# Attention's output projection as seven block products ahead of the raw gate products, with the gates' sums made during the attention

## The chip, the cores and the metric

The kernel runs on one core of a Trainium2 chip. The metric is the device time of one execution in microseconds. Before the change it is 1419.86 us, the median of 3 runs (1419.58 to 1419.86). Five engines work from queues of their own: PE (TensorE: matmuls and transposes), DVE (VectorE), ACT (ScalarE), POOL (GpSimd) and SP (SyncE). SP, ACT and POOL also issue DMAs. Each engine runs its instructions in the order in which they stand; semaphores hold an instruction until others are done.

## The reference, cut to what matters

One residual block on 1024 tokens of 1024 channels, in float32:

```python
xn = rmsnorm(x, norm1_g[layer])
u = xn @ w_in[layer].astype(f32)
q_sb, k_sb, v_sb, f_raw, i_hg, q_hg, g_hg, gate_sb, gate_hg = jnp.split(u, list(c), axis=-1)
o_sb = stick_breaking_attention(split_heads(q_sb, SB_HEADS), ...)   # 8 heads of 64
o_hg = hgrn2_chunkwise(...)                                         # 4 heads of 128
o_hg = rmsnorm(o_hg, ...)
o_hg = merge_heads(o_hg) * jax.nn.silu(g_hg)
g_a = jax.nn.sigmoid(gate_sb + bg[:D_MODEL])
g_b = jax.nn.sigmoid(gate_hg + bg[D_MODEL:])
merged = g_a * (o_sb @ w_o_sb) + g_b * (o_hg @ w_o_hg)
h = x + merged @ w_out
hn = rmsnorm(h, norm2_g[layer])
h = h + jnp.square(jax.nn.relu(hn @ w_ff1)) @ w_ff2
return rmsnorm(h, final_g)
```

The change touches `o_sb @ w_o_sb` (1024 x 512 by 512 x 1024), the columns of `u` that become `g_a` and `g_b`, and where the sums of their inputs and weights are made.

## The kernel before

Every float32 product is made of three matmuls, on a high and a low part of both operands (`three`): high by high, high by low, low by high. `hi_lo` makes the two parts, a cast on ACT and a subtraction on DVE. A matmul takes 128x128 weights and 128x512 moving data; a "step" of the planner is six of them. Several large products are computed as block products with sums of blocks as operands, seven in place of eight, so the sums have to be made beforehand, by DVE or by accumulating DMAs.

The stages follow each other: norm of x and the first projections; the stick-breaking attention (8 heads, 75 to 330 us in the profile); the recurrence HGRN2 (4 heads, about 330 to 555 us); the gates with the output projection of the recurrence (`gates`); the output matrix; the MLP.

In the attention and in the recurrence PE has two lanes. "main" is the work of the stage; "fill" is work that is not urgent: projections and gate products, held in a list of jobs (`Stream`, `st`). `st.advance(n, upto)` issues n steps of the list but none past job `upto`; `st.finish(upto)` issues all up to there. In the recurrence `FILL` says how many steps go behind each piece of main work, and `upto` how far the list may run in each of five rounds. A round is `hg_levels(h)`, the scores of one head at seven levels, beside `hg_tail(h - 1)`, the output of the head before. So the order of the jobs in the list and the `upto` of each round set what stands between two pieces of main work.

Names that the prediction uses:
- `half(...)`: a 128x512 buffer out of a ring of `N_HALF = 10`; it is handed on when all that read the last content are done, a DMA to memory included. `slot(...)`: 128x1024, 40 of them.
- In `hg_levels`, level l: ACT copies the keys to a half (`ksl2_3` is head 2, level 3; line 1092), PE multiplies (`sl`), DVE and ACT lay the result into `sc`, and DVE scales k and q for the next level.
- In `hg_tail`: `pk` and `pkv` make the states, `pho{h}_{half}` the output, ACT takes squares and sums (`hon`, line 1272), POOL the root (`hn_y`, line 269), DVE the product (`hon`, line 169), PE the transposes `pot{h}_{half}`.
- `raw_job(cb)`, the raw gate products of eight column blocks: `pga` (two halves one after the other in one bank) and `pgq`; `p1` and `p14` go to memory (`pd`), `g1`, the sigmoid, to `gd`.
- `sb_job(cp)`, four jobs behind the raw gates: `pys`, two column blocks each, first half times `g1` read back from `gd`, second half plain, both to `yd`. The fourth job runs inside `gates` (`SB_HELD`).
- `sum_forms` and `whole_input`: the sums of the gates' inputs, made between the `pys` steps; the high parts are added to the low ones in place by eight accumulating DMAs (`xnl<-xnh`).
- `gates`: for each of eight pairs the products `x6`, `y5`, `x7`, `y3` (banks gX and gY), on summed inputs and summed weights.

Of the kernel before, what the change touches and what calls it, by code (L numbers as in the profile page):

```python
# [2 lines left out]

# [36 lines left out]
def kernel(  # L40
# [404 lines left out]
    class Unit:  # L445


        late = False
# [54 lines left out]
    class Stream:  # L503
        def __init__(self, eager=False):
            self.eager = eager
            self.jobs = []
            self.pos = 0
            self.gen = None
            self.steps = 0
            self.owed_t = None  # L510
# [14 lines left out]
        def prefetch(self):  # L525
            nxt = []
            for us, _ in self.jobs[self.pos + 1 :]:
                nxt += [u for u in us if u.hl is None]
                if len(nxt) >= 2:
                    break  # L530
            if nxt:
                nxt[0].split()
                if nxt[0].late and not self.jobs[self.pos][0][-1].late:
                    self.owed_t = nxt[0]
                else:
                    nxt[0].split_t()
            if len(nxt) > 1:
                nxt[1].load()

        def step(self):  # L540
# [12 lines left out]
            if next(self.gen, StopIteration) is StopIteration:  # L553
                self.gen = None
                self.pos += 1
            return True
# [657 lines left out]
    def hg_tail(h):  # L1214
# [19 lines left out]
        st.finish(j_i)  # L1234
        open_block("main")
# [72 lines left out]
    a_sb, a_hg = Split("asb"), Split("ahg")  # L1308
# [38 lines left out]

    def gate_bias(which, cb):
        return prm[:, BG + which * KT + cb : BG + which * KT + cb + 1]

    def gate_cols(which, cb):
        if cb < KT:
            c0 = (C_GA, C_GB)[which] + cb * P
        else:
            c0 = C_GH + (2 * (cb - KT) + which) * P
        return slice(c0, c0 + P)

    class RawUnit(Unit):
# [5 lines left out]
        def __init__(self, cb):  # L1364
            dmas = [
                [(0, P, W_IN[:, gate_cols(w, cb)].rearrange("(k p) c -> p k c", p=P))]
                for w in range(2)
            ]
            super().__init__(f"wga{cb}", dmas)
            if cb < KT:  # L1370
                self.roomy = (1,)

        def split(self):
            if self.hl is not None:
                return
            self.load()
            ra, rb = self.raw
            h, l = (
                wpool.tile([P, 1024], F32R, tag=t, name=f"{self.name}{t}") for t in ("whi", "wlo")
            )  # L1380
            hi_lo(h, l, ra)
            self.hl = [(h, l)]

        def split_t(self, behind=None, upto=3):
            ra, rb = self.raw
            while self.turned < upto:
                self.turned += 1
                if self.turned == 1:
                    after(sub(rb, ra, rb), behind)
                elif self.turned == 2:  # L1390
                    after(sub(rb[:, 512:], rb[:, 512:], rb[:, 0:512]), behind)
                else:
                    t = slot(f"{self.name}t", F32R)
                    self.hl.append((t[:, 0:512], t[:, 512:]))
                    after(hi_lo(*self.hl[1], rb[:, 512:]), behind)
# [3 lines left out]
    def raw_job(cb):  # L1399
        u = raw_units[cb]  # L1400

        def steps_of(ps, wt, w0, half_, k0, start):
            wh, wl = u.hl[wt]
# [8 lines left out]

        def body():
            p1, p14, g1 = (half(f"{n}_{cb}") for n in ("p1", "p14", "g1"))
            ps, p4 = bank(f"pga{cb}"), bank(f"pgq{cb}")
            if 6 <= cb < KT:
                load_g1(cb - 6)
            if 5 <= cb < KT:
                sb_units[cb - 5].load()
            if 3 <= cb < KT - 1:  # L1420
                osb[cb - 3] = slot(f"osr{cb}")
                load(osb[cb - 3], od[cb - 3])
            yield from steps_of(ps, 0, 0, 0, 0, True)
# [5 lines left out]
            yield from steps_of(p4, 1, 0, 1, 4, True)  # L1429
            add(p14, p1, p4)  # L1430
            if cb == 3 or cb == KT - 1:
                whole_input(1, int(cb == KT - 1))
            nc.gpsimd.dma_start(pd[cb][:, 1, :], p14)
            yield from steps_of(ps, 0, 4, 0, 4, False)
            if cb < KT:
                nc.scalar.activation(g1, ps, AF.Sigmoid, bias=gate_bias(0, cb))
            else:
                nc.scalar.activation(g1, ps, AF.Sigmoid)
                mul(g1, ps, g1)
            nc.scalar.dma_start(gd[cb], g1)  # L1440
            if 4 <= cb < KT:
                a_sb.put(cb - 4, osb.pop(cb - 4))
# [3 lines left out]
    side, g1r = [], {}  # L1446
# [5 lines left out]
    forms, whole = {}, {}  # L1452
    WAIT = 7

    def whole_input(i, j):
        for kp in range(2):
            h, l = (t.bitcast(F32) for t in xn.t[i, 2 * j + kp])
            nc.gpsimd.dma_start(l, h, accum_op=ALU.add)
            whole[i, j, kp] = l

    def sum_forms():


        raw = whole
        def split(m, kp, src):
            forms[m, kp] = tuple(slot(f"gs{n}{m}{kp}", F32R) for n in "hl")
            hi_lo(*forms[m, kp], src)

        for j in range(2):
            whole_input(0, j)  # L1470
        yield from range(WAIT)
        s1, s2 = {}, {}
        for kp in range(2):
            s1[kp] = slot(f"gs1{kp}")
            ins = add(s1[kp], raw[1, 0, kp], raw[1, 1, kp])
            if kp == 0:
                after(ins, hg_sum[0])
            yield
        for kp in range(2):
            split(5, kp, s1[kp])  # L1480
            yield
        for kp in range(2):
            s2[kp] = slot(f"gs2{kp}")
            sub(s2[kp], s1[kp], raw[0, 0, kp])
            yield
            split(6, kp, s2[kp])
            yield
        gates_in[0].load()
        gates_in[0].load_sums()
        for kp in range(2):  # L1490
            s3 = slot(f"gs3{kp}")
            sub(s3, raw[0, 0, kp], raw[1, 0, kp])
            split(7, kp, s3)
            yield
        gates_in[0].split()
        for kp in range(2):
            s4 = slot(f"gs4{kp}")
            sub(s4, raw[0, 1, kp], s2[kp])
            split(3, kp, s4)
            yield  # L1500
        gates_in[1].load()

    sb_units = []

    def sb_job(cp):
        src = W_OSB[:, cp * 256 : (cp + 1) * 256].rearrange("(k p) c -> p k c", p=P)
        unit = Unit(f"wo0{cp}", [[(0, 256, src)]])
        unit.roomy = (0,)
        sb_units.append(unit)

        def body():
            if cp == 0:
                side.append(sum_forms())
            for j in range(2):
                cb = 2 * cp + j
                if 1 < cb + 1 < KT:
                    load_g1(cb + 1)
                g1 = g1r[cb]
                for i, cs in halves():
                    ps = bank(f"pys{cb}_{i}")  # L1520
                    for _ in proj_half(
                        ps, unit.hl[0], a_sb.mov, 4, i, lambda k: k * 256 + j * P
                    ):
                        next(side[0], None)
                        yield
                    if i == 0:
                        mul(g1, ps, g1)
                        nc.gpsimd.dma_start(yd[cb][:, i, :], g1)
                    else:
                        y = half(f"ys{cb}")  # L1530
                        nc.scalar.copy(y, ps)
                        nc.scalar.dma_start(yd[cb][:, i, :], y)

        return st.add([unit], body)
# [17 lines left out]
    j_raw = [raw_job(cb) for cb in range(KT)]  # L1552
    j_sb = [sb_job(cp) for cp in range(4)]

    class GatePair:
# [3 lines left out]
        def load(self):  # L1559
            cb = self.cb  # L1560
            self.raw = [
                wpool.tile([P, 1024], F32, tag="raw", name=f"wg{cb}r{i}") for i in range(2)
# [26 lines left out]
        def split(self, behind=None):  # L1589
# [4 lines left out]
            after(sub(r0[:, s0], r0[:, s1], r0[:, s0]), first)  # L1594
            sub(r1[:, s0], r1[:, s1], r0[:, s0])
# [8 lines left out]
            sub(r0[:, s1], r1[:, s1], r0[:, s1])  # L1604
# [33 lines left out]
        def gated(self, which, first, second):  # L1638
# [11 lines left out]
            if which == 0:  # L1650
                muls()
# [16 lines left out]
        def x7(self):  # L1668
            self.product(7, self.X, False)
            p1, p14 = self.p[:, 0:512], self.p[:, 512:1024]  # L1670
            self.y_sum = add(p1, p1, self.Y)
            add(p1, p1, self.X)
# [15 lines left out]
        def y3(self):  # L1688
            self.product(3, self.Y, False)
            add(self.u2, self.u2, self.Y)  # L1690
# [52 lines left out]
    SB_HELD = {KT: 4}  # L1743
# [7 lines left out]
    def gates():  # L1751
        for v, n, m in zip(gates_in, gates_in[1:] + [None], gates_in[2:] + [None] * 2):
# [8 lines left out]
            st.advance(SB_HELD.get(v.cb, 0), j_sb[3])  # L1761
# [4 lines left out]
            st.finish(j_sb[3])  # L1766
# [632 lines left out]
    wsums = out_weight_sums()  # L2399
    done = 0  # L2400
    for i, it in enumerate(items):
# [52 lines left out]
    st.finish(j_sb[2])  # L2454
    for _ in side[0]:
# [100 lines left out]
```

## Time and profile before

| | |
|---|---|
| median of the runs | 1419.86 us |
| the profiled execution | 1420.01 us |
| its span, first to last instruction | 1418.2 us |
| granted TensorE clock, mean | 0.999 |
| DVE busy, attention (75 to 330 us) | 186.8 of 255 us |
| DVE busy, 420 to 510 us | 71.6 of 90 us |
| data moved by DMA | 241.91 MB |

All durations below come from that one execution; its own time is 1.8 us over its span. In rows of the timeline and of the groups stand start and duration in microseconds, the engine, the line of the program, the operation, what it writes and reads, the shape, and in brackets how long the engine sat idle before and what ended that. In the chain in order of time a row is start, duration, engine, bank and the number of instructions. In the rows by stretch stand the stretch, its length, then busy time and number of instructions of PE, of PE's weight loads, DVE, ACT and POOL, the granted clock, the DMA engines' busy share and GB/s (where the view is asked for PE alone, the other engines are missing). A row of DMA issues ends with the median time from issue to landing.

### The profile page before, as it was taken

Reading aid. Unit: us, or ns where it says so; the run is one execution under the profiler, and the core shown is the slowest. Engines: PE = TensorE matmul, PEld = TensorE weight load, DVE = VectorE, ACT = ScalarE, POOL = GpSimd, SP = SyncE. Lnnn points to the kernel's source line nnn. Section 1 sums busy time; section 2 is a strip of 40 time slices with the busy share of each in tenths; the row PEclk is TensorE's granted clock in tenths of the full one; section 3 lists DMA queues with packets and bytes.
Section 4 is the critical chain, followed back from the end, with each engine's and each line's share of the span. In section 5 each row is a group of like instructions: output and inputs, shape, how many; then the busy total and the mean of one; then the engine's idle time right before and its main releaser. Section 6 shows DMA issues by size and latency. Waiting matters only on the chain.

```text
span 1418.2 us, 18602 instructions
## 1 busy us (share of the span) xinstructions
PE 1408.0 (99%) x6848; PEld 1183.5 (83%) x6848; DVE 1049.5 (74%) x1429; ACT 659.3 (46%) x1127; POOL 145.0 (10%) x282
## 2 busy tenths in 40 slices
PE   9999999999999999999999999999999999999998
PEld 7888888888888888888888888888888888888886
DVE  6667777778567888887788897676766657668765
ACT  6455555554243554433244764445444443534343
POOL 3011223110011031000000300000000000000042
PEclk9999999999999999999999999999999999999999
DMA  8344445435135685364585514444446974776725
GB/s 253 83 119 127 104 101 102 104 77 154 60 75 169 224 223 186 120 214 156 162 298 194 186 53 170 163 163 142 138 145 239 351 269 148 278 274 242 273 97 186
DMA packets 169730, 241.91 MB, mean 171 GB/s; under 512 B 30844, under 2 KB 97960, under 8 KB 169640
## 3 DMA queue, kind: packets, MB, share of 16 engines
q1 hardware_dynamic: 151432, 192.48, 41.0%
q0 software_dynamic: 11616, 34.61, 9.9%
q10 hardware_dynamic: 6592, 13.63, 2.7%
q8 instruction: 54, 0.88, 0.3%
q14 instruction: 36, 0.29, 0.1%
HBM read 170.43 MB, written 68.16 MB: 168 GB/s over the span
## 4 chain that ended last, share of the span: by engine, by line
PE 97%; ACT 1%; DMA 1%; DVE 1%; issue 0%; POOL 0%; SPq 0%; POOLq 0%; DVEq 0%; ACTq 0%
PE pm L128 21%; PE pX L128 9%; PE pW L128 6%; PE pY L128 6%; PE pjqk L128 6%; PE pga L128 4%; PE gX L128 4%; PE gY L128 4%; PE pjf L128 3%; PE pjq L128 3%; PE pys L128 3%; PE pji L128 3%; PE pyh L128 3%; PE po L128 3%; PE z L128 2%; PE pwX L128 2%
## 5 line engine op out<-in xcount | busy, mean ns | idle before, releaser
L854 DVE TENSOR_TENSOR_SCAN rm<-rm,bits 128x512 f32<-128x512 f32 (+6 forms) x72 | 87.5, 1222 | 30.5 <-ACT rm L835 29.0
L156 ACT CAST whid<-w 128x1024 fp32r<-128x1024 f32 x30 | 31.6, 1054 | 153.8 <-PE pm L128 85.4
L128 PE MATMUL pm<-wlod,sh 128*128 128x512 f32 x240 | 93.6, 390 | 0.0
L128 PE MATMUL pm<-whid,sl 128*128 128x512 f32 x240 | 93.5, 389 | 0.0
L128 PE MATMUL pm<-whid,sh 128*128 128x512 f32 x240 | 93.4, 389 | 0.0
L128 PE MATMUL pm<-tl,sh 128*128 128x512 f32 (+1 forms) x210 | 81.3, 387 | 0.0
L128 PE MATMUL pm<-th,sl 128*128 128x512 f32 (+1 forms) x210 | 81.3, 387 | 0.0
L128 PE MATMUL pm<-th,sh 128*128 128x512 f32 (+1 forms) x210 | 81.3, 387 | 0.0
L161 DVE TENSOR_TENSOR wlod<-w,whid 128x1024 fp32r<-128x1024 f32 x30 | 36.7, 1222 | 55.0 <-ACT whid L156 54.8
L156 ACT CAST wTh<-pw 128x512 fp32r<-128x512 f32 (+2 forms) x96 | 43.7, 482 | 62.4 <-PE pw L131 60.8
L161 DVE TENSOR_TENSOR wTl<-pw,wTh 128x512 fp32r<-128x512 f32 (+2 forms) x96 | 50.5, 548 | 28.9 <-ACT wTh L156 28.6
L161 DVE TENSOR_TENSOR sl<-sa,sh 128x1024 fp32r<-128x1024 f32 x56 | 68.2, 1218 | 0.6 <-ACT sh L156 0.6
L2173 POOL TENSOR_SCALAR fss<-fss 128x1 f32<-128x1 f32 x8 | 4.3, 543 | 562.0 <-ACT fsc L2168 561.5
L156 ACT CAST sh<-sa 128x1024 fp32r<-128x1024 f32 x56 | 57.2, 1045 | 7.8 <-DMA sa<-ad 7.8
L128 PEld LDWEIGHTS pm<-wlod,sh 128*128 128x128 f32 x240 | 45.1, 188 | 9.9 <-DVE wlod L161 0.4
L128 PEld LDWEIGHTS pm<-whid,sh 128*128 128x128 f32 x240 | 45.0, 188 | 9.4
L128 PEld LDWEIGHTS pm<-whid,sl 128*128 128x128 f32 x240 | 45.1, 188 | 9.2
L128 PE MATMUL pX<-sqh,t1l 128*128 128x512 f32 x128 | 50.0, 390 | 0.0
L128 PE MATMUL pX<-sql,t1h 128*128 128x512 f32 x128 | 50.0, 390 | 0.0
L128 PE MATMUL pX<-sqh,t1h 128*128 128x512 f32 x128 | 49.8, 389 | 0.0
L128 PEld LDWEIGHTS pm<-th,sh 128*128 128x128 f32 x210 | 39.5, 188 | 8.1
L128 PEld LDWEIGHTS pm<-tl,sh 128*128 128x128 f32 x210 | 39.4, 188 | 8.0
(936 smaller groups left out, 4358.8 us busy)
## 6 DMA issues: line engine op xcount, KB each, us to landing
w<-in_w_ff_dram SPq DMA_DIRECT2D x72, 512.0 KB, 4.8
sa<-ad SPq DMA_DIRECT2D x52, 512.0 KB, 6.8
ad<-a SPq DMA_DIRECT2D x32, 256.0 KB, 4.5
ad<-s SPq DMA_DIRECT2D x16, 512.0 KB, 3.2
tw<-in_w_out_dram POOLq DMA_DIRECT2D x24, 256.0 KB, 5.8
pr<-pd SPq DMA_DIRECT2D x10, 512.0 KB, 5.8
x<-in_x_dram SPq DMA_DIRECT2D x8, 512.0 KB, 7.9
xnl<-xnh POOLq DMA_DIRECT2D x8, 512.0 KB, 6.2
```

Of the source, the lines that this page charges most:

```text
L128: return pe(nc.tensor.matmul(*a, **k))
L156: hi_last[0] = after(in_turn("act", nc.scalar.copy(dst, src)), hi_behind[0])
L161: nc.vector.tensor_tensor(out=dst, in0=src, in1=hi.bitcast(F32), op=ALU.subtract),
L854: sc = nc.vector.tensor_tensor_scan(out=rr, data0=rr, data1=bits[:, 1024 - nk + a : 1024 - nk + b][:, ::-1], initial=rm[:, b : b + 1] if i ...
L2173: nc.gpsimd.tensor_scalar(out=ssq, in0=ssq, scalar1=1.0 / D, scalar2=EPS, op0=ALU.mult, op1=ALU.add)
```

## The change

The output projection is now seven block products over a 2x2 split (`SB_ORDER` 2, 5, 1, 6, 7, 4, 3), with four column blocks (`cp`) each of six matmuls: 168 matmuls in place of 192. It stands ahead of all eight raw gate products in the list of jobs (`j_sb` ahead of `j_raw`). The products are combined in halves a2, a5, a6 and stored to `yd` before the gate is known; `last` in the raw gate product reads them back (`y0`) and multiplies. Its weight sums (`tv`) and the fourth weight sums of the gates (`tg4`) are made by DMAs on POOL's queue during the attention, and the sums of the gates' inputs (`xs`, stored to `sx`) by 20 DVE operations of 128x1024 during the attention. The raw gates run in the order `RAW_ORDER`; the second-half products of the last four (`HELD`) run inside `gates`, in place of the last quarter of the projection. The signs of several sums in the gates are turned with that. The core of the diff:

```diff
+    def input_sums():
+        def step(out, a, b, op):
+            after(nc.vector.tensor_tensor(out=out, in0=a, in1=b, op=op), turn_lo[0])
+        def stored(m, kp, t):
+            nc.gpsimd.dma_start(sx[m][kp], t)
         for kp in range(2):
...
+            s = slot(f"xs{kp}")
+            step(s, h00, h10, ALU.subtract)
+            yield
...
+            stored(7, kp, s)
...
+    SB_ORDER = (2, 5, 1, 6, 7, 4, 3)
...
+        def end(m, cp, ps):
+            if m in (2, 5, 4):
+                t = half(f"a{m}{cp}")
+                nc.scalar.copy(t, ps)
+                if m == 4:
+                    nc.scalar.dma_start(yd[cp][:, 1, :], t)
+                    return
+                sb_sum[m, cp] = t
+            elif m == 1:
+                t = sb_sum.pop((2, cp))
+                add(t, t, ps)
+                nc.gpsimd.dma_start(yd[cp][:, 0, :], t)
+            elif m == 6:
+                t = sb_sum[6, cp] = half(f"a6{cp}")
+                sub(t, sb_sum[5, cp], ps)
+            elif m == 7:
+                t = sb_sum.pop((5, cp))
+                sub(t, t, ps)
+                nc.gpsimd.dma_start(yd[cp + 4][:, 1, :], t)
+            else:
+                t = sb_sum.pop((6, cp))
+                add(t, t, ps)
+                nc.gpsimd.dma_start(yd[cp + 4][:, 0, :], t)
...
+            for m in ms:
+                n = SB_ORDER.index(m)
+                ahead = SB_ORDER[n + 1 : n + 3]
+                for cp in range(4):
+                    end(m, cp, product(m, cp))
...
+        def last(ps, hl, w0):
+            yield from steps_of(ps, hl, w0, 0, 4, False)
+            g1 = half(f"g1_{cb}")
+            if cb < KT:
+                nc.scalar.activation(g1, ps, AF.Sigmoid, bias=gate_bias(0, cb))
+                mul(g1, g1, y0.pop(cb))
+                nc.gpsimd.dma_start(yd[cb][:, 0, :], g1)
...
-    j_raw = [raw_job(cb) for cb in range(KT)]
-    j_sb = [sb_job(cp) for cp in range(4)]
+    j_sb = [sb_job(ms) for ms in ((2, 5), (1, 6, 7, 4, 3))]
+    j_raw = [raw_job(cb) for cb in RAW_ORDER]
+    j_held = held_job()
...
-    SB_HELD = {KT: 4}
+    SB_HELD = {KT: 4, KT + 1: 5}
...
-        if i % 2 == 1:
+        if i % 16 != 0:
             next(wsums, None)
+        if i > 2 and i % 5 > 1:
+            next(insums, None)
...
-        upto = (j_i, j_raw[1], j_raw[6], j_sb[1], j_sb[2])[h]
+        upto = (j_i, j_sb[0], j_raw[1], j_raw[6], j_raw[7])[h]
...
-    st.finish(j_sb[2])
-    for _ in side[0]:
+    st.finish(j_raw[7])
+    for _ in st.side:
         pass
     gates()
```

How the rows of instructions moved. PE, in the recurrence at head 2, level 2 (`sl_2`; pga is the raw gate product). Before:

```order
L128 MATMUL pga_4433<-xnh_261,wga1whi 128x512
L128 MATMUL pga_4433<-xnl_262,wga1whi 128x512
L128 MATMUL sl_2_4494<-q_3623,ksl_2_4492 128x128 x4
L128 MATMUL pga_4433<-xnh_261,wga1wlo 128x512
L128 MATMUL pga_4433<-xnh_261,wga1whi 128x512
```

PE at the same level now (pys_4577 is product 1, column block 1, and pys_4604 its block 2; the six matmuls of block 0 stand directly ahead of the six of block 1):

```order
L129 MATMUL pys_4577<-asl_4313,wo1whi 128x512
L129 MATMUL pys_4577<-ash_4312,wo1wlo 128x512
L129 MATMUL sl_2_4594<-q_3689,ksl_2_4592 128x128 x4
L129 MATMUL pys_4604<-ash_4312,wo1whi 128x512
L129 MATMUL pys_4604<-asl_4313,wo1whi 128x512
```

Raw gate matmuls around the level have become matmuls of product 1.

ACT at the same place, with what each row waits for (an engine's name, DMAHW for a DMA issued by SP or ACT, DMASW for one issued by POOL; `a` are the halves of the projection). Before:

```order
L156 CAST wga2whi<-wga2r_4366 128x1024 [waits DMAHW2_49]
L1425 DMA pd_112<-p_1_4430 128x512 [waits Activation_49]
L156 CAST wga2t<-wga2r_4368 128x512 [waits DMAHW4_49,DVE_49]
L1092 COPY ksl_2_4492<-k_3370 128x2x64x4
L1436 ACTIVATE g_1_4432<-pga_4433,prm 128x512 [waits PE_49]
L1440 DMA gd_122<-g_1_4432 128x512 [waits Activation_49]
```

And now:

```order
L157 CAST wo6whi<-wo6r 128x1024 [waits DMAHW5_49,PE_49]
L1688 COPY a_4542<-pys_4535 128x512 [waits PE_49]
L157 CAST ash_4719<-osr_4188 128x512 [waits DVE_49]
L1279 ACTIVATE hon_0_4546,hss_0_4545<-pho_0_4544 128x128 [waits PE_49,Activation_49,Pool_49]
L1279 ACTIVATE hon_0_4546,hss_0_4545<-pho_0_4544 128x128 x3
L157 CAST ash_4719<-osr_4196 128x512
L1097 COPY ksl_2_4592<-k_3438 128x2x64x4 [waits DMASW3_49,DVE_49]
L157 CAST wo7whi<-wo7r 128x1024 [waits DMAHW6_49,PE_49]
```

The copy for level 2 had no wait of its own and now has one for a DMA of POOL's queue; by the semaphore's count that DMA is the store of a20 (product 2 plus product 1, column block 0) to `yd`. The copy for level 3 waits in the same way for the store of a50 (product 7, column block 0).

PE at the end of the recurrence, head 3. Before, 18 pys stand between pho_1 and pot_0, and 12 between pot_0 and pot_1, which ends:

```order
L128 MATMUL pys_1_5519<-asbh_5121,wo02h_5237 128x512
L128 MATMUL pys_1_5519<-asbl_5122,wo02h_5237 128x512
L128 MATMUL pys_1_5519<-asbh_5121,wo02l_5238 128x512
L131 MATMUL pot_1_5535<-ident,hon_1_5465 128x128 x4
L128 MATMUL gX_5541<-gsh_5323,whig_5433 128x512
```

Now:

```order
L129 MATMUL pho_1_5580<-v_3861,sc_4906 128x128
L129 MATMUL pho_1_5580<-k_4217,q_4338 128x128
L132 MATMUL pot_0_5614<-ident,hon_0_5544 128x128 x4
L132 MATMUL pot_1_5620<-ident,hon_1_5582 128x128 x4
L129 MATMUL gX_5642<-gsh_5346,whig_5499 128x512
L129 MATMUL gX_5642<-gsl_5347,whig_5499 128x512
```

No fill is left between pho_1, the two groups of transposes and the first gate product.

More of the change, by code (lines that the diff above doesn't have):

```diff
@@ L2 @@
 from contextlib import ExitStack
+from itertools import chain
 import concourse.bass as bass
@@ L555, in step @@
                 self.pos += 1
+            next(self.side, None)
             return True
@@ L1503 @@
[L1503 to L1509, printed above, removed]
-        def body():
[L1512 to L1534, printed above, removed]
+    forms = {}
@@ new lines, in sb_load, with sb_split @@
+    def sb_load(m):
+        plain = {1: (0, 0), 2: (1, 0), 3: (1, 1)}
+        sums = {5: 1, 7: 3, 6: 2, 4: 4}
+        src = sb_block(*plain[m]) if m in plain else tv[sums[m]]
+        sb_raw[m] = wpool.tile([P, 1024], F32, tag="raw", name=f"wo{m}r")
+        load(
+            sb_raw[m].rearrange("p (k c) -> p k c", k=2),
+            src.rearrange("(k p) c -> p k c", p=P),
+        )
+    def sb_split(m):
+        sb_w[m] = tuple(
+            wpool.tile([P, 1024], F32R, tag=t, name=f"wo{m}{t}") for t in ("whi", "wlo")
+        )
+        hi_lo(*sb_w[m], sb_raw.pop(m))
@@ L2453 @@
             st.finish(max(j_f[h + 1], j_q[h + 1]))
-    st.finish(j_sb[2])
-    for _ in side[0]:
+    st.finish(j_raw[7])
+    for _ in st.side:
         pass
```

308 lines of the change are left out of this document (229 added, 79 removed).

## The prediction

> **What bounds the kernel now.** I read the page first, then who waits for what on PE, then busy time by stretch, then the chain in order of time, then the DMA landings.
>
> ```profile
> span 1418.2 us, 18602 instructions
> ...
> PE 1408.0 (99%) x6848; PEld 1183.5 (83%) x6848; DVE 1049.5 (74%) x1429; ACT 659.3 (46%) x1127; POOL 145.0 (10%) x282
> ...
> PE 97%; ACT 1%; DMA 1%; DVE 1%; issue 0%; POOL 0%; SPq 0%; POOLq 0%; DVEq 0%; ACTq 0%
> ```
>
> The profiled execution took 1420.01 us, 1.8 us more than its span; the median of the three runs shown is 1419.86. PE is busy 99% of the span and is 97% of the chain that ended last. Its waits are all at the start:
>
> ```profile
> PE warm L128 <- POOL ident masks.py:199: 2.3, 1, 2.3
> PE xnt L131 <- DVE x L653: 0.4, 1, 0.4
> ```
>
> The stretches that the change touches are full, by busy time for each of the engines:
>
> ```profile
> 75.00:330.00 255.00, 254.94 (x1456) 220.72 (x1455) 186.82 (x244) 143.55 (x327) 55.48 (x134) 1.00 0.49 109
> 420.00:510.00 90.00, 90.00 (x487) 77.14 (x486) 71.59 (x117) 41.02 (x92) 13.72 (x20) 1.00 0.65 193
> 510.00:600.00 90.00, 90.00 (x442) 75.44 (x441) 75.63 (x107) 42.27 (x73) 10.74 (x15) 1.00 0.61 182
> ```
>
> The first bracketed pair is PE: 90.00 of 90. So the kernel gets shorter only by PE work removed, and any new wait on PE is paid in full, since nowhere later does PE have idle time to give it back. The question is thus: how many matmuls go, and where does PE wait in the new order.
>
> **Matmuls removed.** Before, the attention's output projection is 8 column blocks x 2 halves x 12 = 192 matmuls of 128x512. Seven products x 4 column blocks x 6 = 168 replace them. The rest of PE's program has the same instructions, moved. The price, from the chain in order of time (the row with 24 matmuls), with the end of the recurrence stage, which is needed below:
>
> ```profile
> 545.40 1.78 PE pho L128 x16
> 547.18 4.10 PE pys L128 x18
> 551.28 0.44 PE pot L131 x4
> 551.72 2.77 PE pys L128 x12
> 554.49 0.44 PE pot L131 x4
> ...
> 560.40 5.44 PE pys L128 x24
> ```
>
> 24 matmuls cost 5.44 us (0.2267 each): **-5.44 us**. A group of six is 1.36 us.
>
> **Work added in the attention.** Twenty sums of 128x1024 on DVE for the gates' inputs, 8 stores of 512 KB and 24 DMAs of weight sums on POOL's queue. DVE has 255.00 - 186.82 = 68.2 us free there, and such a sum costs
>
> ```profile
> 447.42 1.22 DVE L1317 TENSOR_TENSOR wga3r<-wga3r,wga3r 128x1024 f32<-128x1024 f32 x1
> ```
>
> 1.22 us, so 24 us in all: the free time hides it. One sum can come ahead of a product that PE is about to need, but only when PE's cover there is below 1.22 us. I take +0.4, between 0 and 2.5 (two sums in full at bad places). The POOL issues stand on an engine that is 22% busy there, and nothing of the stage reads what they write.
>
> **Waits added behind stores.** This is the main term. The new products end in halves (128x512 buffers), and ten halves serve everything: a2, a5, a6, the copies of k for the recurrence's levels (ksl), hon. A half that is stored to yd through POOL's queue is free when the store has landed. In the new order ACT's copy of k for level 2 of head 2 carries a wait on POOL's DMA queue: its half is a20's, which DVE finishes only after product 1, block 0, and PE wants that level after one more group of six. The copy for level 3 gets the half of a50, two groups of six behind product 7, block 0. Before, the same kind of wait is harmless:
>
> ```profile
> 432.24 0.58 POOL L1433 DMA_DIRECT2D pd<-p  x1 [11.56 <-DVE k L1249]
> ...
> 448.94 0.65 ACT L1092 COPY ksl<-k 128x512 f32<-128x512 f32 x1
> ```
>
> The store stands 16.7 us ahead of the copy that takes its half. Now the hand-offs, row by row:
>
> ```profile
> 444.06 0.68 DVE L1314 TENSOR_TENSOR p<-p,pgq 128x512 f32<-128x512 f32 x1
> 445.04 0.63 POOL L1433 DMA_DIRECT2D pd<-p  x1 [2.76 <-DVE p L1314]
> ...
> 458.01 0.61 ACT L1092 COPY ksl<-k 128x512 f32<-128x512 f32 x1
> 458.67 1.16 PE L128 MATMUL sl<-q,ksl 128*128 128x128 f32 x8
> ```
>
> DVE's sum takes 0.68, POOL issues 0.30 after its end (445.04 - 444.74), ACT's copy takes 0.61, PE starts 0.05 behind it (458.67 - 458.62): 1.64 us beside the landing. The landings of 256 KB through POOL's queue, asked for 425 to 445, 445 to 460, 460 to 480 and 480 to 500 us:
>
> ```profile
> pd<-p POOLq DMA_DIRECT2D x1, 256.0 KB, 4.1
> ...
> pd<-p POOLq DMA_DIRECT2D x2, 256.0 KB, 5.7
> ...
> pd<-p POOLq DMA_DIRECT2D x2, 256.0 KB, 4.0
> ...
> pd<-p POOLq DMA_DIRECT2D x1, 256.0 KB, 2.3
> ```
>
> Weighted, (4.1 + 11.4 + 8.0 + 2.3) / 6 = 4.3 us.
> Level 2: 1.64 + 4.3 - 1.36 = 4.6. Ahead of a20's sum DVE also has a 128x1024 and a 128x512 operation queued, 1.22 + 0.68 = 1.9 us if it is behind, 0 if not; DVE is 80% busy there before (71.59 of 90) and gets more work, so I add 1.2: **+5.8 us** (2.6 with a landing of 2.3 and no queue, 7.9 with 5.7 and the whole queue). Behind this copy on ACT stand the cast of the next weights and hon's squares; both have more than a group of six to go, so they shift with PE.
> Level 3: 1.64 + 4.3 - 2.72 = **+3.2 us** (1.2 to 5.3, with one 0.68 ahead).
> Three more places wait for such stores with a cover about as long as the chain (a63 ahead of product 7's last block, the copy for level 5, hon of head 1): **+0.8 us** together (0 to 1.5).
>
> **A wait at the end of the recurrence.** hon is the normed output of a half of a head: squares on ACT, root on POOL, product on DVE. Before, 30 pys matmuls and four transposes stand between the last pho and the second pot (547.18 to 554.49). In the new order pot_0, pot_1 and the gates follow pho_1 directly, so PE waits for hon less the four transposes. The shortest and the longest such latency:
>
> ```profile
> 438.08 1.56 PE pho L128 x14
> ...
> 442.32 0.69 DVE L169 TENSOR_TENSOR hon<-pho,hn_y 128x512 f32<-128x512 f32 x1 [3.63 <-ACT wga2whi L156]
> ...
> 552.71 0.69 DVE L169 TENSOR_TENSOR hon<-pho,hn_y 128x512 f32<-128x512 f32 x1 [0.93 <-POOL hn_y L269]
> ```
>
> 442.32 + 0.69 - 439.64 = 3.37, and 553.40 - 547.18 = 6.22. Less 0.44: 2.9 to 5.8. The long one had two casts of 128x1024 among its squares, and in the new order ACT has none there, so I take the short side: **+3.2 us**.
>
> **What moves without a price.** Half of the second-half products of the raw gates (48 matmuls) moves into the gates, where a quarter of the output projection (48 pys matmuls) stood: PE does as much there as before, and the gates' own order around it is the same. Their products with y0 need a load of 256 KB from yd that SP issues one block of 12 matmuls (2.72 us) or more ahead; nothing on PE waits for their result but a bank. If that load were late by its whole landing it would hold DVE, which is not full in that stretch (75.63 of 90), and PE only behind it, so I cost it at 0. The removed accumulating DMAs, subtractions and g1 traffic all stood beside a full PE: 0.
>
> **The sum.** -5.44 + 0.4 + 5.8 + 3.2 + 0.8 + 3.2 = +8.0 on 1420.01: **1428.0 us**, 0.6% slower. All low ends: -5.44 + 0 + 2.6 + 1.2 + 0 + 2.9 = +1.3, 1421.3. All high ends: -5.44 + 2.5 + 7.9 + 5.3 + 1.5 + 5.8 = +17.6, 1437.6.
>
> **The rivals.**
> Short landings: with every store near the 2.3 of one row, levels 2 and 3 cost 3.8 and 1.2 and the near ties nothing: -5.44 + 0.4 + 3.8 + 1.2 + 3.2 = +3.2, 1423.2. For it: the DMA engines carry less then, since raw gate loads come later. Against: five of six rows. [...]
>
> The clock falls while PE waits. These are PE's busy time, matmuls and granted clock at both ends of the span:
>
> ```profile
> 3.00:4.00 1.00, 1.00 (x7) 1.00 1.04 401
> ...
> 5.00:6.00 1.00, 1.00 (x9) 1.00 1.11 282
> ...
> 1412.00:1418.20 6.20, 0.00 (x0) 0.76 0.59 209
> ```
>
> After the last matmul the granted clock means 0.76 over 6.20 us; if the lower step is a half, it fell for 0.24 x 6.20 / 0.5 = 3.0 us, so some 3.2 us into the idle time. A level-2 wait of 5.8 us is longer. At the start PE does 7 matmuls in a microsecond and later 9, so a restart costs some 0.7 us, and up to 1.6 at half speed for 3.2 us: 1428.0 + 1.5 = 1429.5. Against it: the clock is recorded as 1.00 in that start, so the price is not shown. [...]
>
> The ring has a free half: if levels 2 and 3 get halves whose stores landed long ago, as the row of 16.7 us shows for the kernel before, both waits are gone and the near ties too: -5.44 + 0.4 + 3.2 = -1.8, 1418.2, not slower. It decides at a cover of 1.64 + 4.3 = 5.9 us between store and use; the new order has 1.36 and 2.72, which speaks against it.
>
> No new wait binds at all: -5.4, 1414.6. That would need the pot wait hidden too, against a shortest latency of 3.37.
>
> **Chances.** Forecast 0.45, clock 0.22, short landings 0.17, free half 0.08, no wait 0.08. A measurement of this kernel tells about 0.2% from no change, 2.8 us: same is 1417.0 to 1422.7. Faster is the last rival and a little of the free half: 0.09. Same is most of the free half and half of the short landings: 0.16. Slower is the rest, 0.75. The range goes from the free half, 1418, to 1434, six above the forecast: the clock and half of the high ends together. It leaves out the no-wait case and some 0.1 above.
>
> **What would show it.** In the new profile, PE's waits should have rows for sl behind ksl, 8 to 10 us in two long pieces, and for pot behind hon, about 3 us, and ACT's ksl should wait for DMA of yd. The attention should end where it does now. If PE's waits stay at the start only, the forecast is wrong as a whole; if they are there but short, the landing was mis-sized; if the clock is below 1.00 after a wait, the clock rival is right.

## The result, and the profile after

The changed kernel takes 1439.41 us, the median of 4 runs (1438.11 to 1440.66), beside 1419.86 (1419.58 to 1420.27) for the kernel before: a ratio of 1.0137, interval 1.012 to 1.0155. It is 1.4% slower. The prediction was 1428.0 in a range of 1418 to 1434: slower was right, the size was not, and the time lies outside the range. The profiled execution took 1438.38 us, so 18.4 more than that of before, with a span 18.0 longer.

The page of the changed kernel, with the span, the busy times and the chain's shares by engine:

```profile
span 1436.2 us, 18699 instructions
...
PE 1409.7 (98%) x6824; PEld 1182.0 (82%) x6824; DVE 1066.1 (74%) x1463; ACT 667.9 (47%) x1147; POOL 165.4 (12%) x318
...
PE 93%; ACT 2%; DMA 2%; issue 1%; DVE 1%; POOL 1%; SPq 0%; POOLq 0%; ACTq 0%; DVEq 0%
```

24 PE instructions are gone, as the change says. But PE is 93% of the chain where it was 97%, and ACT and DMA, with 2% each, have twice their share. Its waits (total, how often, the longest):

```profile
PE sl L129 <- ACT ksl L1097: 11.3, 5, 4.8
PE pot L132 <- DVE hon L170: 3.0, 1, 3.0
...
PE po L129 <- DVE wTl L162: 0.8, 1, 0.8
```

The three stretches that were full before (busy times of PE, PE's loads, DVE, ACT, POOL; then clock, DMA share, GB/s):

```profile
75.00:330.00 255.00, 253.91 (x1449) 219.35 (x1448) 203.39 (x260) 143.24 (x325) 78.47 (x166) 1.00 0.76 173
420.00:510.00 90.00, 81.06 (x409) 67.95 (x408) 66.78 (x113) 39.05 (x77) 10.71 (x19) 0.96 0.42 138
510.00:600.00 90.00, 84.60 (x431) 70.53 (x430) 64.70 (x102) 44.86 (x94) 10.59 (x18) 0.98 0.59 196
```

PE now idles 1.1, 8.9 and 5.4 us in them, 15.4 in all, which agrees with the waits in the view above (15.1). The granted clock is below 1.00 in the last two. The five waits of `sl`, one row each in the timeline (start, duration; the bracket is PE's idle time before):

```profile
436.73 1.18 PE L129 MATMUL sl<-q,ksl 128*128 128x128 f32 x8 [0.94 <-ACT ksl L1097]
...
448.25 1.16 PE L129 MATMUL sl<-q,ksl 128*128 128x128 f32 x8 [3.25 <-ACT ksl L1097]
...
468.25 2.08 PE L129 MATMUL sl<-q,ksl 128*128 128x128 f32 x8 [4.75 <-ACT ksl L1097]
...
532.66 1.16 PE L129 MATMUL sl<-q,ksl 128*128 128x128 f32 x8 [1.28 <-ACT ksl L1097]
...
540.83 1.16 PE L129 MATMUL sl<-q,ksl 128*128 128x128 f32 x8 [1.09 <-ACT ksl L1097]
```

The first three are levels 1, 2 and 3 of head 2, the last two levels of head 3. What held them, by the chain in order of time (start, duration, what):

```profile
444.90 2.60 DMA yd<-a
...
447.58 0.63 ACT ksl L1097
...
462.48 5.03 DMA yd<-a
...
467.58 0.63 ACT ksl L1097
...
470.33 0.85 PE pot L132 x4
471.18 3.99 PE pys L129 x11
...
565.74 1.15 ACT hon L1279 x8
...
568.32 0.70 DVE hon L170
...
569.07 0.66 PE pot L132 x4
569.72 4.33 PE gX L129 x12
```

Both long waits of head 2, levels 2 and 3, go through a store to `yd` that has to land before ACT may overwrite its half, and the wait of `pot` goes through the squares, the root and the product of `hon`. These are the three places that the prediction named. (`pot` and `pys` at 470 us come right behind the eight `sl` of 468.25.) But those eight take 2.08 us behind the wait at level 3 and 1.16 behind the one at level 2. The rows of PE alone show why (length, PE busy and matmuls, clock, DMA share, GB/s; the lower six are cut where PE starts or stops and where the clock changes):

```profile
444.90:447.50 2.60, 0.10 (x1) 1.00 0.76 292
462.48:467.51 5.03, 1.02 (x5) 0.99 0.90 294
...
463.50:467.39 3.89, 0.00 (x0) 1.00 1.00 332
467.39:474.22 6.83, 5.97 (x20) 0.50 0.05 19
474.22:477.00 2.78, 2.78 (x14) 1.00 0.27 100
...
569.07:569.79 0.72, 0.72 (x5) 1.00 1.04 399
569.79:573.21 3.42, 3.42 (x10) 0.50 1.10 362
573.21:576.00 2.79, 2.79 (x14) 1.00 0.15 57
```

The clock fell to a half at 467.39, while PE waited, and came back only at 474.22. Behind the wait of `pot` it fell too, from 569.79 to 573.21, although PE had started again at 569.07. What that costs follows from the chain: 2.08 + 0.85 + 3.99 = 6.92 us at level 3, against 0.89 (eight `sl` at full clock, seen in an experiment below) + 0.44 + 11 x 0.2267 = 3.82, so 3.1; and 0.66 + 4.33 against 0.44 + 12 x 0.2267 at `pot`, 1.8.

The other three waits of `sl` have no store ahead of them. They stand behind ACT's own queue, here in the timeline for the two of head 3 (at level 1 it is a copy out of `pys` and two casts):

```profile
531.41 0.69 ACT L1460 ACTIVATE g<-pga,prm 128x512 f32<-128x512 f32 x1 [0.71 <-PE pga L129]
532.00 0.61 ACT L1097 COPY ksl<-k 128x512 f32<-128x512 f32 x1
...
539.22 1.04 ACT L157 CAST gsh<-gs 128x1024 fp32r<-128x1024 f32 x1
540.15 0.62 ACT L1097 COPY ksl<-k 128x512 f32<-128x512 f32 x1
```

No copy has idle time of ACT before it (no bracket): ACT was busy with a gate's sigmoid, which itself had waited for the gate's product (0.71), and a cast of the gates' inputs.

In the rows by stretch above, the first two are the two landings. The longer one, 5.03 us, moved over a DMA system that was 90% busy, the shorter one, 2.60 us, over 76%.

The end of the program. After the last matmul the changed kernel has 7.90 us (1428.30 to 1436.20) and the kernel before 6.40 (1411.80 to 1418.20), with the same work: DVE, ACT and POOL are busy 2.0, 2.4 and 1.3 us in it, before 2.0, 2.5 and 1.3. What differs is a DRAIN on POOL's queue, an instruction that stands behind all of POOL's work. Before, in the changed kernel, and in the run below in which SP issues the stores of products 1 and 7 (a row has the number of such instructions, the shortest, median and longest in ns, the first and last start in us):

```profile
L2551 POOLq DRAIN  x3: 46/102/2516, 1413.1 to 1417.9; - x3
...
L2758 POOLq DRAIN  x3: 46/102/5823, 1429.6 to 1436.0; - x3
...
L2758 POOLq DRAIN  x3: 50/93/5166, 1431.5 to 1437.2; - x3
```

The long one lasts 2.5 us where POOL issues 133 DMAs in the program, 5.8 where it issues 169, and 5.2 with 161. In the changed kernel it ends at 1435.4, behind SP's wait for the last output, which is over at 1434.4. Before it ended at 1415.7, and SP's wait came last, at 1417.4. So the longer end goes with the 36 DMAs that POOL issues more; why the DRAIN grows with them the runs don't show.

**Where the 18.0 us of span come from:**

| | predicted | measured |
|---|---|---|
| 24 matmuls removed | -5.4 | -5.4 |
| attention (idle 1.09 less 0.06) | +0.4 | +1.0 |
| head 2, level 1 (in the prediction: near ties) | +0.8 | +0.9 |
| head 2, level 2 | +5.8 | +3.3 |
| head 2, level 3 | +3.2 | +4.8 |
| head 3, two levels | 0 | +2.4 |
| `pot` behind `hon` | +3.2 | +3.0 |
| clock at a half behind two waits | 0 | +4.9 |
| behind the last matmul | 0 | +1.5 |
| sum | +8.0 | +16.4 |

The rest, 1.6 us, is mostly PE's restart behind a wait at full clock: at level 2 eight `sl` take 1.16 us and not 0.89, so 0.27 each time, for some five waits.

### The profile page after: what moved, and what is told of

The parts are those of the page before. It is cut to its first block, busy times and chain, and to the rows that moved or that the text cites. A ratio compares the mean times of both kernels' runs of the same rounds, so it can differ in the third digit from the quotient of the medians.

```text
span 1436.2 us, 18699 instructions
## 1 busy us (share of the span) xinstructions
PE 1409.7 (98%) x6824; PEld 1182.0 (82%) x6824; DVE 1066.1 (74%) x1463; ACT 667.9 (47%) x1147; POOL 165.4 (12%) x318
## 4 chain that ended last, share of the span: by engine, by line
PE 93%; ACT 2%; DMA 2%; issue 1%; DVE 1%; POOL 1%; SPq 0%; POOLq 0%; ACTq 0%; DVEq 0%
PE pm L129 21%; PE pX L129 9%; PE pW L129 6%; PE pY L129 6%; PE pjqk L129 5%; PE gX L129 4%; PE pga L129 4%; PE gY L129 4%; PE pjf L129 3%; PE pji L129 3%; PE pyh L129 3%; PE pjq L129 3%; PE po L129 3%; PE pwX L129 2%; PE pjv L129 2%; PE z L129 2%
## 5 line engine op out<-in xcount | busy, mean ns | idle before, releaser
L840 ACT ACTIVATE rm<-z 128x512 f32<-128x512 f32 (+3 forms) x96 | 44.3, 498 | 7.0 <-DMA sx<-xs 4.2
```

Of the source, the lines that this page charges most:

```text
L840: scored[0] = nc.scalar.activation(rm[:, s0 : s0 + m], z[:, :m], AF.Sigmoid, scale=-0.125)
```

## The experiments

The theory is the prediction's, corrected in size: the halves that wait for stores (8 us at two levels), the clock behind the second of them, the lost cover of `hon`, the DVE sums of the attention. The main rival is that a wait only moves when its cause is taken away. A question beside it is what makes a landing long, the queue or the place. Each ratio is against the kernel before on the same chip. In these kernels some line numbers are one higher than in the changed one.

### Keys in halves of their own

```diff
-    N_FULL, N_HALF = 40, 10
+    N_FULL, N_HALF = 39, 10
...
+    kpool = ctx.enter_context(tc.tile_pool(name="keys", bufs=2))
...
-            keys = slot_n(f"k{name}", 512)
+            keys = kpool.tile([P, 512], F32, tag="k", name=f"k{name}")
```

> The copies of k for the recurrence's levels get two halves of their own; one full buffer less pays for them (39 instead of 40); all else as in the change. Theory (the copies of levels 2 and 3 of head 2 wait for a half whose store has to land): the two long waits of PE for sl, 3.4 and 4.9 us, are gone, and with the second one the half clock behind it (2.9 us): 11.2 us less than the change, about 1428. Rival (the copies are late because ACT, DVE or POOL are late there, and the store only ends last): another wait takes their place, less than 4 us gained.

1427.36 us (1426.3 to 1428.31), ratio 1.0053 (1.0036 to 1.007): 12 us less than the changed kernel, from one decision on buffers. No wait of `sl` is left, and the clock holds where it had been halved; a row of PE alone:

```profile
468.00:470.00 2.00, 2.00 (x15) 1.00 0.99 389
```

So the halves do cause the waits of head 2. Those of head 3 go too, but there the trace shows another order on ACT: the copies for the two levels (523.24 and 527.54 in this run) now stand ahead of the sigmoid (524.04) and of the cast (530.69), and not behind them. What remains in PE's waits is the lost cover of `hon`, and two new ones in the attention:

```profile
PE pot L133 <- DVE hon L171: 3.0, 1, 3.0
...
PE pjq L130 <- DVE wTl L163: 2.2, 1, 2.2
PE z L130 <- ACT osb L935: 1.3, 1, 1.3
```

The chain shows how these two come about (the last row, from the recurrence, is that of eight `sl` at full clock):

```profile
150.12 8.88 DMA sx<-xs
...
159.14 5.36 DMA od<-osb
...
165.37 1.91 PE pjq L130 x6
...
457.85 0.89 PE sl L130 x8
```

Behind the wait of `pjq` the clock fell once more: six `pjq` take 1.91 us in place of 1.36 and the next twelve 3.40 in place of 2.72, and the mean granted clock over the attention is 0.99 here and 1.00 in the changed kernel. The keys' space came out of the ring of 40, and with 39 the attention waits for a store of an input sum. That was tried by itself, next.

### One 128x1024 buffer fewer, nothing else

The edit is `N_FULL` 39 alone.

> The change with 39 full buffers instead of 40 and nothing else. Theory (the first experiment's attention ended later because the 40th full buffer is needed there, by the sums of the input): about 4 us slower than the change, some 1443, all of it before 330 us. Rival (that delay came from the moved order of issue and not from the buffer): the same as the change, 1439.

1442.73 us (1439.35 to 1443.4), ratio 1.0155 (1.014 to 1.0171), 3.3 above the changed kernel. In the stretch of the attention PE is busy 250.74 of 255 us, against 253.91 in the changed kernel: 3.2 us. So the loss in the attention above belongs to the buffer. Between the two kernels with 39 buffers, with and without halves for the keys, lie 15.4 us.

### Keys in one half, taken from the ring of halves

The same pool with `bufs=1`, and `N_HALF` 9, so that no other ring shrinks.

> The change with one half of its own for the copies of k and nine in the ring: the memory of the change exactly, 40 full buffers. Theory (the shared ring is the cause, and the attention of the first experiment lost some 4 us to the missing full buffer): the waits for levels 1 to 3 of head 2 and the half clock are gone and the attention is that of the change: 1439 - 1.1 - 3.4 - 4.9 - 2.9 = about 1427, or 1424 if the two waits of head 3 go too, as they did in the first experiment. Rival (nine halves are too few for a2, a5, a6 and hon): DVE or ACT wait for stores there and PE behind them, over 1431.

1432.54 us (1431.29 to 1433.96), ratio 1.0089 (1.0074 to 1.0104): the rival, in part. The keys don't wait any more. Instead ACT waits for halves of `hon` (6.7 us in two waits) and DVE for a half of product 6 (2.7), each held by a store, and PE waits behind DVE at product 7:

```profile
PE pys L130 <- DVE a L1325: 5.8, 3, 2.9
```

5.8 us of waits in place of 8.0, and no more: whoever takes a half out of this ring next has to wait for a landing. It is the number of halves against the time that a store holds one, not the keys as such.

### No sums of the gates' inputs

```diff
-            s = slot(f"xs{kp}")
-            step(s, h00, h10, ALU.subtract)
...
+            for m, src in ((7, h00), (6, h10), (3, h01), (5, h11)):
+                for _ in range(2):
+                    yield
+                stored(m, kp, src)
+                yield
```

> The change without the 20 sums of 128x1024 on DVE in the attention; eight stores of 512 KB remain, but of plain parts of the input, so that the gates get unsummed inputs. Theory (one such sum stands ahead of a wTl and of a q that PE waits for at 167 and 161 us): the attention ends 1.1 us earlier, as before the change, about 1438.3. Rival (the DMAs of the sums, which nearly double the traffic there, are what is late): no gain.

1438.09 us (1436.92 to 1438.56), ratio 1.0128 (1.0113 to 1.0143), 1.3 below the changed kernel, whose runs and these overlap. PE is busy 254.94 of 255 us in the attention, as before the change. That says more than the two medians, for in this run's profile the clock also fell behind level 2 (eight `sl` in 2.08 us), which it did not in the changed kernel's. In the changed kernel the place is (timeline)

```profile
164.84 1.21 DVE L1522 TENSOR_TENSOR xs<-xs,xnl 128x1024 f32<-128x1024 f32 x1
165.98 1.21 DVE L162 TENSOR_TENSOR wqk5l<-wqk5r,wqk5h 128x1024 fp32r<-128x1024 f32 x1
167.11 0.87 DVE L162 TENSOR_TENSOR wTl<-pw,wTh 128x512 fp32r<-128x512 f32 x2
167.84 0.38 PE L129 MATMUL po<-wTl,V 128*128 128x256 f32 x1 [0.79 <-DVE wTl L162]
```

One of the twenty sums stands ahead of a subtraction that PE waits for, on an engine that is 80% busy (203.39 of 255). The other nineteen cost nothing that shows.

### Cover for the normed output at the end of the recurrence

`FILL` of the last round from 2.9 to 1.9, which leaves fill matmuls between the last `pho` and `pot`.

> The change with 1.9 in place of 2.9 steps of fill per piece in the last round of the recurrence, so that 12 of the 48 raw gate matmuls left there stand between the last pho and the first pot, and 6 between the two pots (4.1 us). Theory (hon's latency has no cover): PE's wait for hon of 3.15 us is gone, and the half clock behind it (1.7 us): 4.9 us less, about 1434.5. Rival (the products taken away ahead of pkv and pho uncover waits there): less than 3 us gained, with new waits for pp or k.

1435.89 us (1434.88 to 1437.21), ratio 1.0114 (1.0099 to 1.0129): 3.5 below the changed kernel, where 4.9 were expected. The wait of `pot` and the fall of the clock behind it are gone (the clock is 1.00 over 510 to 600 us). Of the other 1.4, 1.0 stands in its waits as two new ones, `pkv` behind ACT (0.7) and the gates' `gX` behind DVE (0.3): the fill that was moved had covered them.

### Matmuls in place of the idle time

Twenty matmuls of 128x512 into the bank of level 3, meant to keep PE busy through the wait there.

```diff
+            for _ in range(20 if name == "sl2_3" else 0):
+                matmul(S, ones, xn.mov(0, 0)[0], start=True, stop=True)
```

> The change, with 20 matmuls of 128x512 on operands that are ready, put on PE directly ahead of head 2's level 3, into the bank that the level then overwrites: 20 x 0.2267 = 4.5 us of PE work that falls into the 4.9 us wait. Theory (the matmuls of 0.43 us behind that wait come from the granted clock, which falls because PE is idle): the clock stays at 1.00 there and the 2.9 us are gone, about 1436.5. Rival (they are slow because of what DVE, ACT and the DMAs do then): the same slow matmuls, no gain, or a loss where the wait is shorter than 4.5 us.

1442.82 us (1442.35 to 1445.04), ratio 1.0166 (1.0151 to 1.0181). This says nothing on the question, for the order of PE's program did not put them where they were meant to be. In its timeline (the second row; the first is level 2) they stand ten microseconds ahead of the wait:

```profile
447.58 2.08 PE L129 MATMUL sl<-q,ksl 128*128 128x128 f32 x8 [3.09 <-ACT ksl L1097]
...
458.65 4.70 PE L129 MATMUL sl<-xnh,ones 128*128 128x512 f32 x20
```

The wait at level 3 (4.43 us) and the half clock (0.50 from 472 to 476 us) stayed, and the 20 matmuls came on top. The run shows something else by chance: the wait at level 2, here 3.09 us, is followed by eight `sl` in 2.08 us, so the clock fell, which it did not behind 3.25 us in the changed kernel's profile. The last section has the rows of both.

### Stores by SP in place of POOL

```diff
-                nc.gpsimd.dma_start(yd[cp][:, 0, :], t)
+                nc.sync.dma_start(yd[cp][:, 0, :], t)
...
-                nc.gpsimd.dma_start(yd[cp + 4][:, 1, :], t)
+                nc.sync.dma_start(yd[cp + 4][:, 1, :], t)
```

> The change, with the eight stores of products 1 and 7 to yd issued by SP in place of POOL; the ring and the order of the products as in the change. Theory (the two long waits are the store's landing and little else: landings of 2.6 and 5.0 us gave waits of 3.4 and 4.9): with SP's stores near the 2.0 to 2.7 of its other stores of 128 to 256 KB the second wait falls to some 2.5 us and no longer drops the clock: 2.4 + 2.9 less, about 1434; the first stays near 3. Rival (the landing depends on what the DMA engines carry then, not on the queue; or SP, held by the wait for DVE, brings the next weights late): no gain, or new waits for loads.

1439.48 us (1437.61 to 1439.62), ratio 1.0135 (1.012 to 1.015): no gain in the time. The chain's two landings:

```profile
445.70 2.92 DMA yd<-a
...
464.71 4.71 DMA yd<-a
```

2.92 and 4.71 where POOL's queue had 2.60 and 5.03: at these two places the landing hardly depends on the queue. The equal time is a sum of small things. In this run's profile the wait at level 3 is 0.6 shorter and the end 0.7, but the attention idles 1.0 more, and the clock fell behind level 2 as well (a wait of 3.05, then eight `sl` in 2.07).

### The causes taken together

First the keys in one half and `FILL` 2.4 in each of the last three rounds.

> One half of its own for the copies of k, nine in the ring, and 2.4 steps of fill per piece in the last three rounds of the recurrence (2.6, 2.6, 2.9 in the change), so that 24 raw gate matmuls stand between the last pho and the last pot. Theory (ring and fill are all that the change lacks): no wait of PE over 1 us from 330 to 600 us and the clock at 1.00: 1427 less 4.9 for hon and its clock, less 2.9 for head 3, about 1419, where the 24 matmuls saved are half spent by the attention's 1.1 and near ties. Rival (with the ring tight, waits only move): over 1424.

1426.75 us (1424.5 to 1428.51), ratio 1.0047 (1.003 to 1.0064), and not 1419. What is left is one wait of 3.0 for the half of product 6's last block, which a store holds (4.90 us in the chain), with twelve `pys` behind it that take 4.60 us where twelve at full clock take 2.72, and small waits. Then also the stores by SP, and the sums of the inputs behind other pieces of the attention (`i % 5 < 3` in place of `i % 5 > 1`).

> The kernel of both ring and fill, with products 1 and 7 stored by SP, and with the sums of the input stepped at the items 0, 1, 2 of each five in place of 2, 3, 4. Theory: the wait of 3.2 us for a63 (its half too waits for a store) falls under 2 us, and the sums no longer stand ahead of the wTl and q of 161 and 167 us (1.9 us): 1426.8 less 1.5 less up to 1.9, about 1424. Rival (the sums hold some other item of the attention instead, and the shorter store only uncovers DVE): 1426 to 1428.

1421.27 us (1419.8 to 1424.04, 10 runs), ratio 1.0011 (1.0001 to 1.002), the clock at 0.999 as before the change. In the attention PE is busy 254.80 of 255 us, with all twenty sums in it. What each of the two edits gives on this kernel was not tried apart. Last, two other fills on top of that, 2.4, 2.5, 2.5 and 2.4, 2.6, 2.1.

> Keys in a half of their own with nine halves in the ring, products 1 and 7 stored by SP, the sums of the gates' inputs behind other pieces of the attention, and FILL 2.4, 2.5, 2.5 (1421.3 us with 2.4, 2.4, 2.4). Head 3 then keeps 18 matmuls between pot_0 and pot_1 and 12 fewer behind pot_1, so the gates start straight behind pot_1. Theory: of what is left over the removed matmuls the two waits of the gates' products for ahgl (1.55 us) come from DVE being late behind a raw gate product that fills the place behind pot_1; they go, and the time is 1419.5 to 1420. Rival: they belong to the gates' own order (they stand some 15 us behind pot_1), then they stay and it is 1421 to 1422; and if PE waits for hon again in front of pot_0 (6 matmuls of cover in place of 12) it is above 1422.

> As the run before it, with FILL 2.4, 2.6, 2.1: 6 matmuls between pho_1 and pot_0, 13 between pot_0 and pot_1, 5 behind it, and 12 or 18 around the levels of heads 2 and 3. Theory: as above with less of it, 1420 to 1421; the halves of product 7, which cost 0.9 us in one wait, may do better with 18 matmuls ahead of level 3 than with 12. Rival: each shift of fill opens a wait elsewhere of the same size, 1421 to 1423. If neither run is under 1417, no order of this fill was found that beats the kernel before.

The first takes 1420.04 us (1419.15 to 1421.93, 11 runs), ratio 1.0005 (0.9996 to 1.0014): as fast as the kernel before. The second takes 1423.84 (1422.79 to 1424.67), ratio 1.0027 (1.0016 to 1.0038): `sl` and `pot` wait again, 1.1 us each. The PE waits of the first:

```profile
PE pyh L130 <- DVE ahgl L163: 1.4, 2, 0.8
PE pys L130 <- DVE a L1325: 0.8, 1, 0.8
PE pX L130 <- DVE u L1322: 0.7, 1, 0.7
```

The time is as the theory gave it, but not for its reason: the waits of `pyh` stayed, as its rival had it. The waits of `pyh` and `pX` are in every profile here with nine halves in the ring (the run with one half for the keys has 0.7 of each) and in none with ten, so they look like a price of the half taken from it; that was not tried. So 24 matmuls fewer, worth 5.4 us, with waits that add up to 2.9 us here, an end longer by 0.9 and restarts give a kernel equal to the one before. No version that beats it was found.

## Why the prediction was wrong in size

**What bounds the kernel.** Right: PE was full, and each new wait was paid in full. The 15.1 us of waits are nearly all of the idle time.

**Matmuls removed.** Right: 24, at 0.2267 us.

**The attention.** The mechanism was right, one sum at one bad place: +1.0 for +0.4, within its ends. The run without the sums shows it.

**Waits behind stores.** The mechanism and the two levels were right, and the sum of both nearly so: 9.0 predicted, 8.0 measured. The step "Weighted, (4.1 + 11.4 + 8.0 + 2.3) / 6 = 4.3 us" gave one landing for both, and they were 2.60 and 5.03. At level 2 the queue on DVE, for which 1.2 was added, was not there; 1.64 + 2.60 - 1.36 = 2.9 of the 3.25, and most of the rest is POOL, which issued the store 0.25 late, behind the root of `hon`. At level 3 a landing of 5.03 makes 1.64 + 5.03 - 2.72 = 3.95 of the 4.75. The other 0.8 is the queue on DVE, which the forecast had only in its high end there: block 0 of product 7 was done at 460.78, and DVE, at the subtraction for the weights of product 4 (`wo4wlo`, 460.36 to 461.58), began with its sum at 461.50.

**Near ties.** +0.8 for 0.9, but by luck: the three places named show no wait, and level 1 has one that was not named, behind ACT's queue.

**"What moves without a price."** Wrong. It priced the moved raw gates by PE, DVE and the loads, with "nothing on PE waits for their result but a bank", and left ACT's order out. Two levels of head 3 wait 2.4 us for ACT's copy, and no store is in it: the copies stand behind the sigmoid of a gate and a cast of 128x1024 there. With the keys in halves of their own the copies stand ahead of both, with the same ACT work, and the waits are gone. So it is ACT's order that made them, though it was not changed by itself.

**The wait for `hon`.** Right: +3.2 for 3.0, and a little fill ahead of `pot` removes it.

**The clock.** This is the largest miss: a rival with a chance of 0.22 and "1428.0 + 1.5 = 1429.5" was true, and true twice, with 3.1 + 1.8 = 4.9 us. The price was bounded by "up to 1.6 at half speed for 3.2 us". That the half would last for 3.2 us was the author's estimate, and no run shows it: at level 3 it lasted 6.83 us, of which PE worked 5.97, and behind `pot` 3.42. And the wait of `pot`, at 3.2 us right beside the 3.2 after which the clock was read to fall, was not counted at all. That reading counts from 1412.0, while the last matmul ended at 1411.8. What spoke against the rival, "the clock is recorded as 1.00 in that start", was a misreading too: in the same trace the 128x128 matmuls of `warm` take 0.42 us each up to 4.8 us and 0.28 from 5.6 us on, so the start was slow though the column says 1.00.

**The end.** +1.5 behind the last matmul, which no part of the prediction looked at: the DMAs added to POOL's queue were priced in the attention only.

The range was too narrow because of what was put at nothing. The waits that had a price (attention, near ties, both levels of head 2, `hon`) add up to 13.4 us in the forecast and 13.0 measured; that the sum fits is partly luck, since level 2 was too long and level 3 too short. The 10 us that were missed are the clock (4.9), the two levels of head 3 (2.4), the end (1.5) and the restarts (most of 1.6), and the range had room for one fall of the clock at 1.5.

## What to carry to other kernels

A buffer that leaves through a DMA was held until the landing, 2.60 and 5.03 us at the two levels here, so moving a store-heavy stage next to a latency-bound one is a question of how many buffers the ring has times how long a store holds one; look for the next user of each buffer, and give the stage on the critical path a buffer of its own before touching anything else (12 us here, 15 with the other buffers equal). Where PE is full, count the clock behind a wait as well: here a wait of 3.0 us cost 1.8 more in half clock and one of 4.75 us 3.1 more. And cover that was free in the old order (fill between the last product and its transposes) has to be counted as part of what is moved.

## What the runs showed of the hardware that was not expected

The clock fell behind some waits of PE and not behind others of nearly the same length. The wait at level 2 of head 2, 3.05 to 3.25 us long, is in six profiles, and the clock fell behind it in five of them. It stayed in the changed kernel, where the wait is the longest of the six. The rows of PE alone, in the changed kernel and, with a wait of 3.09, in the run with twenty matmuls more:

```profile
445.00:447.00 2.00, 0.00 (x0) 1.00 0.93 362
447.00:449.00 2.00, 0.75 (x6) 1.00 0.34 131
449.00:451.00 2.00, 2.00 (x12) 1.00 0.00 0
...
445.00:447.00 2.00, 0.00 (x0) 1.00 0.56 213
447.00:449.00 2.00, 1.42 (x6) 0.55 0.34 131
449.00:451.00 2.00, 2.00 (x9) 0.60 0.00 0
```

In the other four the waits are 3.21 (no sums of the gates' inputs), 3.18 (cover for the normed output), 3.21 (39 buffers) and 3.05 (stores by SP), and in rows of 2 us the clock goes down to 0.50, 0.57, 0.50 and 0.50. So the length of the wait alone does not decide between them; what does was not shown.

Nor did the fall always lie in the wait. In the changed kernel it came 0.86 us ahead of PE's start at level 3 (467.39 and 468.25), and 0.72 us behind it at `pot` (569.79 and 569.07). The half then lasted 6.83 and 3.42 us (rows in the section on the result), and the longer one cost 3.1 us and the shorter one 1.8; what ended them was not shown.

The changed kernel's runs also differ more (1438.11 to 1440.66) than those of before (1419.58 to 1420.27), and the two slower ones have a mean clock of 0.994 and the two faster ones 0.995; that the wait at level 2 decides between them is likely, but was not shown.
